# Output projections of a hybrid decoder trunk in weight blocks of 512 rows by 512 columns

## The chip, the cores and the metric

The kernel runs on one core of one Trainium2 chip. The metric is the device time of one execution in microseconds (us), as the median of the runs. The core's engines are TensorE (PE, matmuls), VectorE (DVE), ScalarE (ACT), GpSimd (POOL) and SyncE (SP, which here issues nearly all transfers). Each runs its own list of instructions in order and waits on semaphores for the others.

## What is computed

A trunk of two residual layers and a final RMSNorm on x of 1024 tokens by 1024 channels, in float32. Each layer ends with an output projection, and that is what the change is about:

```python
def rmsnorm(x, w):
    xf = x.astype(jnp.float32)
    y = xf * lax.rsqrt(jnp.mean(xf * xf, axis=-1, keepdims=True) + EPS)
    return (y * w.astype(jnp.float32)).astype(x.dtype)
```

Layer 0 joins an SSD branch (1024 channels, RMS-normed over all of them) and a differential attention branch (8 heads of 128) to y of 2048 channels; layer 1 is an HGRN2 recurrence with 16 heads of 128, again 2048 channels. Then x = x + y @ w_out with w_out of 2048 rows by 1024 columns, and layer 1 (or the final norm) starts from the RMS norm of that x.

## The kernel before

**Exact products.** Every float32 operand is split into two float32r parts, hi (a cast on ACT) and lo (the difference, on DVE). A product takes three matmuls: hi by hi, hi by lo, lo by hi. In `mm_tm` (matmuls on line 168) the stationary side is 128 channels by 128 tokens of y, the moving side 256 columns of the weights; in `mm_cm` (line 158), used by the input projections, the stationary side is a weight tile and the moving side 512 tokens. Weights come in blocks of 1024 rows by 256 columns through `_wprep`: two transfers of 512 KB into "w_raw" (line 110), two casts into "w_hi" (line 116), two differences into "w_lo" (line 117); "w_hi" and "w_lo" have two buffers each.

**Buffers.** Tiles are taken by tag from a table `SLOTS`, and tiles of all phases share the slots: "A" has 11 of 4 KB per partition, "V" four, "bt", "ey" and "th" one each. A tile can be filled only when the last reader of the slot's tile before is done. PSUM has two banks "pj", two "s1" and two pairs "big".

**The output projection** is `out_proj` (from line 652), called once a layer. The rows of y are transposed tiles of 128 channels by 512 tokens (a half `hf` of the tokens) that were stored in DRAM; `load_y` loads one (into "th" or, for odd tiles of half 1, "ey") or two at once (into "w_raw") and splits them. Part A takes channel tiles 0 to 7, which are there early (in layer 0 the SSD branch), for all tokens: four weight blocks `cb`, per block and half an x1 tile of 512 tokens by 256 columns, loaded from x (line 667) and updated with the sums (line 676 in layer 1; line 680 in layer 0, where the SSD branch's row scale is applied here). Part B takes channel tiles 8 to 15, for half 0 and then half 1, four weight blocks each, so that these blocks are loaded twice. Its sums are added on line 720, squares follow on ACT (723), and the row scale (734) ends in `finish`. In layer 0 `finish` stores x1 and makes layer 1's normed and transposed input; in layer 1 it scales the rows by the final norm and stores them.

**Order.** The code is written in program order and a tile scheduler puts every engine's list together, ahead of time. It draws part A's matmuls into the last heads, where PE would wait for softmax or state updates: they are filler there. A head ends in tail transposes (line 600 in the attention), the product with the gate and a store of its y (`emit_y`, lines 627 and 628). In an HGRN head the running state `st` is in "bt": a copy (1057) and updates (1059) on DVE, and the products with the state on PE (1066), beside the products within the chunk (1064).

## Time and profile before

| | us |
|---|---|
| median of three runs | 2345.65 (2345.0 to 2347.86) |
| the profiled execution, span | 2346.1 |
| PE busy in it | 2262.1 |
| DVE, ACT, POOL busy | 1269.5, 824.8, 187.5 |

The profile is of one execution. An engine's busy time is the union of its instructions; a matmul's listed duration overlaps its neighbours', so that the distance from start to start is its price in a stream. "Releaser" is what ended a wait. Windows give the busy time between two moments, and the granted clock of PE as a share of its full speed: 1.00 is 2.4 GHz and 0.50 is 1.2 GHz.

### The profile page before, as it was taken

The page shows a single profiled execution, that of the slowest core. Times are in us where ns is not written, and L with a number is a line of the kernel's source. Part 1 is how long each engine was busy: PE and PEld are TensorE (multiplying, and loading weights), DVE is VectorE, ACT ScalarE, POOL GpSimd, SP SyncE. Part 2 cuts the span into 40 slices and gives each one's busy share as a digit, 9 for nine tenths or more (in the row PEclk, how much of TensorE's full clock was granted, in tenths as well). Part 3 has the DMA queues.
Part 4 walks back from the last instruction along what each step waited for, and adds up shares of the span by engine and source line. Part 5 has one row for each costly group of instructions (what it writes and reads, how often), then busy time and mean ns, then how long its engine had stood idle before and what let it go on. Part 6 is the DMA issues. An engine that isn't in the chain of part 4 may idle for free.

```text
span 2346.1 us, 40804 instructions
## 1 busy us (share of the span) xinstructions
PE 2262.1 (96%) x16868; PEld 1927.1 (82%) x16868; DVE 1269.5 (54%) x2838; ACT 824.8 (35%) x1887; POOL 187.5 (8%) x201
## 2 busy tenths in 40 slices
PE   6959989899999999999999999999999999999998
PEld 4747766788778787788998888888888888989998
DVE  4736657535554545665444355555646465557444
ACT  4413333224444444544343223332323232334233
POOL 1000111100000000000001010101011010100000
PEclk9979999999999999999999999999999999999999
DMA  5342323231211211231432111111111111124323
GB/s 131 63 78 69 94 73 85 60 82 37 50 46 36 50 39 52 82 128 37 156 123 85 37 55 54 47 46 46 46 46 46 46 50 42 55 65 153 123 94 126
DMA packets 180701, 166.29 MB, mean 71 GB/s; under 512 B 9431, under 2 KB 162401, under 8 KB 180516
## 3 DMA queue, kind: packets, MB, share of 16 engines
q1 hardware_dynamic: 173668, 152.42, 21.5%
q0 software_dynamic: 2624, 7.08, 2.0%
q10 hardware_dynamic: 4224, 4.19, 0.5%
q8 instruction: 132, 2.16, 0.4%
q14 instruction: 53, 0.43, 0.1%
HBM read 132.66 MB, written 26.80 MB: 68 GB/s over the span
## 4 chain that ended last, share of the span: by engine, by line
PE 83%; DMA 10%; DVE 4%; ACT 2%; issue 1%; SPq 0%; POOL 0%; ACTq 0%; POOLq 0%; DVEq 0%
PE pj L158 38%; PE pj L168 21%; DMA G<-acs_d 6%; PE big L545 5%; PE big L168 5%; PE s L581 3%; PE big L976 2%; DMA tz_d<-o 1%; PE s L577 1%; PE big L1064 1%; PE big L1066 1%; PE s L1053 1%; DVE G L442 1%; PE big L1018 1%; DVE w_lo L117 1%
## 5 line engine op out<-in xcount | busy, mean ns | idle before, releaser
L158 PE MATMUL pj<-u,w_hi 128*128 128x512 f32 x3072 | 988.4, 399 | 12.2 <-ACT A L397 8.5
L158 PEld LDWEIGHTS pj<-u,w_hi 128*128 128x128 f32 x3072 | 570.4, 189 | 136.5 <-ACT A L397 9.7
L158 PE MATMUL pj<-u,w_lo 128*128 128x512 f32 x1536 | 609.7, 397 | 0.0
L168 PE MATMUL pj<-w_hi,u 128*128 128x256 f32 x2592 | 496.5, 287 | 1.0 <-DVE A L206 1.0
L168 PEld LDWEIGHTS pj<-w_hi,u 128*128 128x128 f32 x2592 | 409.6, 191 | 9.5 <-issue 5.6
L168 PE MATMUL pj<-w_lo,u 128*128 128x256 f32 x1296 | 370.2, 286 | 0.0
L158 PEld LDWEIGHTS pj<-u,w_lo 128*128 128x128 f32 x1536 | 290.2, 189 | 61.4 <-issue 2.2
L117 DVE TENSOR_TENSOR w_lo<-w_raw,w_hi 128x1024 fp32r<-128x1024 f32 x168 | 204.6, 1240 | 104.4 <-ACT w_hi L116 104.2
L168 PEld LDWEIGHTS pj<-w_lo,u 128*128 128x128 f32 x1296 | 248.0, 191 | 1.7 <-issue 0.6
L116 ACT CAST w_hi<-w_raw 128x1024 fp32r<-128x1024 f32 x168 | 168.0, 1046 | 200.2 <-PE pj L158 113.7
L545 PE MATMUL big<-A 128*128 128x512 f32 (+7 forms) x384 | 142.0, 420 | 0.0
L206 DVE SCALAR_TENSOR_TENSOR A<-th,pj 128x512 f32<-128x512 f32 x80 | 55.0, 688 | 143.9 <-ACT th L205 143.3
L205 ACT ACTIVATE th<-pj 128x512 f32<-128x512 f32 x96 | 57.2, 596 | 207.5 <-PE pj L158 202.7
L559 ACT ACTIVATE p<-p,mx 128x256 f32<-128x256 f32 (+7 forms) x128 | 98.7, 772 | 84.2 <-DVE mx L555 76.4
L545 PEld LDWEIGHTS big<-A 128*128 128x128 f32 (+1 forms) x384 | 71.2, 185 | 58.9 <-issue 50.6
L132 POOL TENSOR_TENSOR ro<-rs_t,mhalf 128x4 f32<-128x4 f32 x48 | 53.2, 1109 | 828.3 <-DVE rs_t L131 663.3
L579 ACT COPY wT<-s 128x512 f32<-128x512 f32 (+2 forms) x96 | 45.9, 478 | 134.4 <-PE s L577 133.9
L442 DVE TENSOR_SCALAR G<-G,ph 128x128 f32<-128x128 f32 x128 | 28.9, 287 | 108.1 <-DMA G<-acs_d 108.1
L893 POOL TENSOR_SCALAR A<-th,fN,fB 128x512 f32<-128x512 f32 x32 | 47.6, 1488 | 470.0 <-ACT th L890 470.0
L581 PE MATMUL s<-V,wT 128*128 128x128 f32 x576 | 81.2, 277 | 0.0
L960 DVE TENSOR_TENSOR A<-A,p 128x512 f32<-128x512 f32 x96 | 65.7, 685 | 23.5 <-PE big L976 23.0
L581 PEld LDWEIGHTS s<-V,wT 128*128 128x128 f32 x576 | 73.8, 191 | 4.5 <-issue 1.6
(328 smaller groups left out, 3030.7 us busy)
## 6 DMA issues: line engine op xcount, KB each, us to landing
w_raw<-in_even_w_in SPq DMA_DIRECT2D x32, 512.0 KB, 4.7
w_raw<-in_odd_w_in SPq DMA_DIRECT2D x64, 256.0 KB, 3.5
w_raw<-in_odd_w_in SPq DMA_DIRECT2D x32, 512.0 KB, 3.9
w_raw<-in_even_w_in SPq DMA_DIRECT2D x48, 256.0 KB, 3.9
w_raw<-in_even_w_out SPq DMA_DIRECT2D x24, 512.0 KB, 4.4
w_raw<-in_odd_w_out SPq DMA_DIRECT2D x24, 512.0 KB, 5.2
G<-acs_d SPq DMA_DIRECT2D x32, 256.0 KB, 4.7
yo<-ey SPq DMA_DIRECT2D x32, 256.0 KB, 2.0
```

The lines of the kernel that those rows point to most:

```text
L116: nc.scalar.copy(hq, raw)
L117: nc.vector.tensor_tensor(lq, raw, hq.bitcast(F32), op=ALU.subtract)
L132: nc.gpsimd.tensor_tensor(dst, t[:, :n], self.mhalf[:, :n], op=ALU.pow)
L158: nc.tensor.matmul(out, lhsT=ww[:, k, ms], rhs=uu[k][:, sl], start=(n == 0), stop=(n == 3 * KT - 1))
L168: nc.tensor.matmul(out, lhsT=uu[k], rhs=ww[:, k, :], start=(k == 0 and j == 0), stop=(k == KT - 1 and j == 2))
L205: nc.scalar.activation(th, pj, AF.Tanh, scale=0.5)
L206: nc.vector.scalar_tensor_tensor(out, view(th), 1.0, view(pj), op0=ALU.add, op1=ALU.mult)
L442: nc.vector.tensor_scalar(R[:, h], R[:, h], S.acs[:, c, 4 * g + h:4 * g + h + 1], 0.0, op0=ALU.subtract, op1=ALU.min)
L545: nc.tensor.matmul(s[:, k0:k0 + kn], lhsT=q[:, isl], rhs=k[:, k0:k0 + kn], start=(j == 0), stop=(j == 1))
L559: nc.scalar.activation(p[:, :n], p[:, :n], AF.Exp, bias=mx, accum_out=z)
L581: nc.tensor.matmul(po[:, i % 4, :], lhsT=wT[:, j * P:j * P + P], rhs=V(j, hh), start=(j == 0), stop=(j == i))
L960: nc.vector.tensor_tensor(k, k, bc(halves(Ts[h], 1)[1], [P, L // (2 * h), h]), op=ALU.mult)
```

## The change

Both projections go through w_out in eight blocks of 512 rows by 512 columns: four row groups `kq` of four channel tiles, two column halves `n`. A sum has 12 matmuls of 512 moving columns, where it had 24 of 256, and is added to x1 after every `kq`, so that each row of x1 is updated four times. The x1 tiles hold 256 tokens by 512 columns. `kq` 0 and 1 run over all tokens in "pj" banks, 2 over all tokens in "big" banks (two token tiles to an eviction). For `kq` 3 both blocks stay on chip, and the tokens go by halves; squares are taken of 512 columns, and in layer 1 each row is scaled and stored as soon as its second column half is done (`finish.row`). Each weight block is loaded once, 8 a layer in place of 12. The x1 tiles keep their list of tags; in the list's last place, "bt", stands now the last tile of the first row group.

```diff
@@ -94,25 +94,27 @@
         n, b = BANKS[tag]
         return self.pp.tile(shape or [P, n * 512], F32, name=tag, tag=tag, bufs=b)
     def _wprep(self, i):
         if i >= len(self.wspecs) or i in self.wtiles:
             return
         nc = self.nc
         src, row0, cols = self.wspecs[i]
-        hi = self.t("w_hi", [P, KT, WB], F32R)
-        lo = self.t("w_lo", [P, KT, WB], F32R)
+        wid = sum(n for _, n in cols)
+        kt = KT * WB // wid
+        hi = self.t("w_hi", [P, kt, wid], F32R)
+        lo = self.t("w_lo", [P, kt, wid], F32R)
         for q in range(2):
-            raw = self.t("w_raw", [P, KT // 2, WB])
-            k0 = q * (KT // 2)
+            raw = self.t("w_raw", [P, kt // 2, wid])
+            k0 = q * (kt // 2)
             o = 0
             for c0, n in cols:
                 nc.sync.dma_start(
                     raw[:, :, o:o + n],
-                    src[row0 + k0 * P:row0 + (k0 + KT // 2) * P, c0:c0 + n].rearrange(
+                    src[row0 + k0 * P:row0 + (k0 + kt // 2) * P, c0:c0 + n].rearrange(
                         "(k p) n -> p k n", p=P))
                 o += n
-            hq, lq = hi[:, k0:k0 + KT // 2, :], lo[:, k0:k0 + KT // 2, :]
+            hq, lq = hi[:, k0:k0 + kt // 2, :], lo[:, k0:k0 + kt // 2, :]
             nc.scalar.copy(hq, raw)
             nc.vector.tensor_tensor(lq, raw, hq.bitcast(F32), op=ALU.subtract)
         self.wtiles[i] = (hi, lo)
@@ -159,16 +161,17 @@
                                  start=(n == 0), stop=(n == 3 * KT - 1))
                 n += 1
-    def mm_tm(self, out, w, uh, ul, ks=range(KT)):
+    def mm_tm(self, out, w, uh, ul):
         nc = self.nc
         wh, wl = w
-        for k in ks:
+        kt = len(uh)
+        for k in range(kt):
             for j, (uu, ww) in enumerate(((uh, wh), (uh, wl), (ul, wh))):
                 nc.tensor.matmul(out, lhsT=uu[k], rhs=ww[:, k, :],
-                                 start=(k == 0 and j == 0), stop=(k == KT - 1 and j == 2))
+                                 start=(k == 0 and j == 0), stop=(k == kt - 1 and j == 2))
 @@ -650,92 +653,78 @@
 def out_proj(S, y_d, wcols, x_d, x1_tags, rs_a, finish):
     nc = S.nc
-    part = lambda y, t: [[z[:, i, t * P:t * P + P] for z in y] for i in range(2)]
     load = lambda hf, k, *tags: load_y(S, y_d, wcols, hf, k, tags)
-    ya, yb = [[], []], [[], []]
+    y = [[], []]
+    part = lambda kq, hf, t: [[z[:, i, t * P:t * P + P] for z in y[hf][4 * kq:4 * kq + 4]] for i in range(2)]
     for hf in range(2):
         for k in range(0, KT, 2):
-            ya[hf] += load(hf, k, "u", "u")
-    x1s = [], []
-    for cb in range(4):
+            y[hf] += load(hf, k, "u", "u")
+    x1s = {}
+    tags = iter(x1_tags)
+    for kq in range(2):
+        for n in range(2):
+            w = S.wnext()
+            for hf in range(2):
+                for t2 in range(2):
+                    if kq == 0:
+                        x1 = x1s[hf, n, t2] = S.t(next(tags), [P, 2, 512])
+                        r0 = hf * 512 + t2 * 256
+                        nc.sync.dma_start(x1, x_d[r0:r0 + 256, n * 512:n * 512 + 512].rearrange(
+                            "(t p) n -> p t n", p=P))
+                    x1 = x1s[hf, n, t2]
+                    for t in range(2):
+                        pa = S.ps("pj")
+                        S.mm_tm(pa, w, *part(kq, hf, 2 * t2 + t))
+                        if rs_a is None:
+                            nc.vector.tensor_tensor(x1[:, t], pa, x1[:, t], op=ALU.add)
+                        else:
+                            tok = hf * 4 + 2 * t2 + t
+                            nc.vector.scalar_tensor_tensor(x1[:, t], pa, rs_a[:, tok:tok + 1], x1[:, t],
+                                                           op0=ALU.mult, op1=ALU.add)
+            if kq == 1 and n == 0:
+                for k in range(KT, KT + 6, 2):
+                    y[0] += load(0, k, "A", "A")
+    for k in range(KT + 6, KT + 8):
+        y[0] += load(0, k, "u")
+    for k in range(8):
+        y[1] += load(1, KT + k, ("V", "V", "G", "G", "p0", "p0", "p1", "wT")[k])
+    for n in range(2):
         w = S.wnext()
         for hf in range(2):
-            x1 = S.t(x1_tags[2 * cb + hf], [P, 4, WB])
-            nc.sync.dma_start(x1, x_d[hf * 512:hf * 512 + 512, cb * WB:cb * WB + WB].rearrange(
-                "(t p) n -> p t n", p=P))
-            x1s[hf].append(x1)
             for t2 in range(2):
-                pa = S.ps("pj", [P, 2, WB])
-                ts_ = slice(2 * t2, 2 * t2 + 2)
+                pb = S.ps("big", [P, 2, 512])
                 for t in range(2):
-                    S.mm_tm(pa[:, t], w, *part(ya[hf], 2 * t2 + t))
-                if rs_a is None:
-                    nc.vector.tensor_tensor(x1[:, ts_], pa, x1[:, ts_], op=ALU.add)
+                    S.mm_tm(pb[:, t], w, *part(2, hf, 2 * t2 + t))
+                x1 = x1s[hf, n, t2]
+                nc.vector.tensor_tensor(x1, pb, x1, op=ALU.add)
+    ws = [S.wnext(), S.wnext()]
+    for hf in range(2):
+        ss = S.sm.tile([P, 4, 2], F32, name="ss4", bufs=2)
+        rows = [x1s[hf, n, t2] for n in range(2) for t2 in range(2)]
+        rss = []
+        for n in range(2):
+            for t in range(4):
+                pa = S.ps("pj")
+                S.mm_tm(pa, ws[n], *part(3, hf, t))
+                xr = x1s[hf, n, t // 2][:, t % 2]
+                nc.vector.tensor_tensor(xr, pa, xr, op=ALU.add)
+                jk = S.t("th", [P, 512])
+                nc.scalar.activation(jk, xr, AF.Square, accum_out=ss[:, t, n:n + 1])
+                if n == 1:
+                    sr = S.sm.tile([P, 1], F32, name="sr")
+                    nc.vector.tensor_tensor(sr, ss[:, t, 0:1], ss[:, t, 1:2], op=ALU.add)
+                    rs = S.sm.tile([P, 1], F32, name="rs")
+                    S.rstd(rs, sr, 1.0 / D, EPS)
+                    rss.append(rs)
+                    finish.row(hf, t, [x1s[hf, m, t // 2][:, t % 2] for m in range(2)], rs)
                 else:
-                    for t in range(2):
...
+                    finish.early(xr)
+        finish(hf, x1s, rss)
 def wspecs(a):
@@ -752,7 +741,7 @@
             specs.append((W, 0, [(AG0 + h * P, WB)]))
         elif h < 7:
             specs.append((W, 0, [(AV0 + (h + 1) * P, WB)]))
-    out = lambda w: [(w, half * D, [(cb * WB, WB)]) for half in (0, 1, 1) for cb in range(4)]
+    out = lambda w: [(w, kq * 512, [(n * 512, 512)]) for kq in range(4) for n in range(2)]
     l0 = specs + out(WO)
     W, WO = a["odd_w_in"][0], a["odd_w_out"][0]
     specs = []
@@ -801,25 +790,30 @@
     nc = S.nc
     def finish(hf, x1s, rs):
-        for cb, x1 in enumerate(x1s):
-            nc.scalar.dma_start(x1_d[hf * 512:hf * 512 + 512, cb * WB:cb * WB + WB].rearrange(
-                "(t p) n -> p t n", p=P), x1)
+        for n in range(2):
+            for t2 in range(2):
+                r0 = hf * 512 + t2 * 256
+                nc.scalar.dma_start(x1_d[r0:r0 + 256, n * 512:n * 512 + 512].rearrange(
+                    "(t p) n -> p t n", p=P), x1s[hf, n, t2])
+        for cb in range(4):
             if hf == 0:
                 xn = [S.t("o", [P, 2, WB]) for _ in range(2)]
             else:
                 xn = S.t("G", [P, 4, WB])
                 xn = [xn[:, 0:2], xn[:, 2:4]]
             for t in range(4):
+                src = x1s[hf, cb // 2, t // 2][:, t % 2, (cb % 2) * WB:(cb % 2) * WB + WB]
                 if t % 2:
-                    nc.scalar.activation(xn[t // 2][:, t % 2], x1[:, t], AF.Copy, scale=rs[t])
+                    nc.scalar.activation(xn[t // 2][:, t % 2], src, AF.Copy, scale=rs[t])
                 else:
-                    nc.vector.tensor_scalar(xn[t // 2][:, t % 2], x1[:, t], rs[t], None, op0=ALU.mult)
+                    nc.vector.tensor_scalar(xn[t // 2][:, t % 2], src, rs[t], None, op0=ALU.mult)
             for j in range(2):
                 k = 2 * cb + j
                 if u[0] is None:
                     u[0], u[1] = S.alloc_u()
                 S.u_block(u, k, hf, [xn[t // 2][:, t % 2, j * P:j * P + P] for t in range(4)], wcol[:, k:k + 1])
-    finish.early = None
+    finish.early = lambda xr: None
+    finish.row = lambda hf, t, x1, rs: None
     return finish
@@ -907,35 +901,30 @@
     for i in range(2):
         fw = S.t("o", [P, 512])
         nc.gpsimd.dma_start(fw, bc(a["final_norm_w"][i * 512:i * 512 + 512].unsqueeze(0), [P, 512]))
-        fws += [fw[:, 0:WB], fw[:, WB:]]
...
+        fws.append(fw)
+    def early(xr):
+        nc.vector.tensor_tensor(xr, xr, fws[0], op=ALU.mult)
+    def row(hf, t, x1, rs):
+        o = S.t("u", [P, D])
+        nc.scalar.activation(o[:, 0:512], x1[0], AF.Copy, scale=rs)
+        nc.vector.scalar_tensor_tensor(o[:, 512:], x1[1], rs, fws[1], op0=ALU.mult, op1=ALU.mult)
+        r0 = hf * 512 + t * P
+        nc.sync.dma_start(out[r0:r0 + P, :], o)
     def finish(hf, x1s, rs):
-        for t in range(4):
...
+        pass
+    finish.early, finish.row = early, row
     out_proj(S, lambda k, n: yo[k:k + n], None, x1_d, ["V", "V"] + ["A"] * 5 + ["bt"], None, finish)
```

Comments taken away by the change are left out here. The two sides of three places in the engines' lists:

PE at the end of layer 0's last head, before. L600 are the last tail transposes (s1_8677); behind and ahead of them are sums of half 0, and the last values stand 65 matmuls further up.

```order
L168 MATMUL pj_9660<-w_hi_9427,A_9424 128x256
L168 MATMUL pj_9660<-w_lo_9428,A_9424 128x256
L168 MATMUL pj_9660<-w_hi_9427,A_9424 128x256
L168 MATMUL pj_9660<-w_hi_9427,u_9647 128x256
L600 MATMUL s1_8677<-ident_71,o_8658 128x128 x4
L168 MATMUL pj_9660<-w_lo_9428,u_9647 128x256
L168 MATMUL pj_9660<-w_hi_9427,u_9647 128x256
L168 MATMUL pj_9660<-w_hi_9427,u_9706 128x256
L168 MATMUL pj_9660<-w_lo_9428,u_9706 128x256
```

The same place now. L584 are the last values (wT_8637), L603 the tail transposes; V_9289, V_9294, G_9299 and G_9304 are channel tiles 8 to 11 of half 1.

```order
L584 MATMUL s1_8515<-V_7030,wT_8637 128x128 x4
L171 MATMUL big_9389<-w_hi_9155,V_9289 128x512
L171 MATMUL big_9389<-w_lo_9156,V_9289 128x512
L171 MATMUL big_9415<-w_hi_9155,V_9289 128x512
L171 MATMUL big_9415<-w_lo_9156,V_9289 128x512
L171 MATMUL big_9389<-w_hi_9155,V_9289 128x512
L171 MATMUL big_9415<-w_hi_9155,V_9289 128x512
L603 MATMUL s1_8677<-ident_71,o_8658 128x128 x4
L171 MATMUL big_9389<-w_hi_9155,V_9294 128x512
L171 MATMUL big_9389<-w_lo_9156,V_9294 128x512
L171 MATMUL big_9415<-w_hi_9155,V_9294 128x512
L171 MATMUL big_9415<-w_lo_9156,V_9294 128x512
```

Between the last values and the transposes there are now six matmuls, and what follows the transposes takes channel tile 9 (V_9294) of half 1; all products of the second column half with half 0's tiles, which were loaded earlier, come later in the list.

SP, the same place before. yb_75<-ey_8682 is the store of the last head's y, th and ey are loads of half 1's channel tiles.

```order
L636 DMA th_10165<-yb_75 128x512
L110 DMA w_raw_9786<-in_even_w_out 128x4x256
L110 DMA w_raw_9790<-in_even_w_out 128x4x256
L628 DMA yb_75<-ey_8682 128x512
L636 DMA ey_9779<-yb_75 128x512
L636 DMA ey_9916<-yb_75 128x512
L110 DMA w_raw_9903<-in_even_w_out 128x4x256
L110 DMA w_raw_9907<-in_even_w_out 128x4x256
```

Now, with ey_9292 for V_9294 and ey_9302 for G_9304:

```order
L112 DMA w_raw_9443<-in_even_w_out 128x2x512
L112 DMA w_raw_9447<-in_even_w_out 128x2x512
L639 DMA th_9297<-yb_75 128x512
L639 DMA th_9307<-yb_75 128x512
L631 DMA yb_75<-ey_8682 128x512
L639 DMA th_9317<-yb_75 128x512
L639 DMA ey_9292<-yb_75 128x512
L639 DMA ey_9302<-yb_75 128x512
```

The loads into "ey" stand behind the store on both sides. Before, all of half 0's part-B products lay between them and their use on PE; now it is the products shown above.

DVE at the end of layer 1's last head, before. bt_19911 is the head's state, pj the part-A sums.

```order
L1057 COPY bt_19911<-s1_19923 128x128
L1059 SCALAR_TENSOR_TENSOR bt_19911<-bt_19911,p1_19730,s1_19923 128x128 x3
L676 TENSOR_TENSOR A_20395<-pj_20397,A_20395 128x512
L1059 SCALAR_TENSOR_TENSOR bt_19911<-bt_19911,p1_19730,s1_19932 128x128 x3
L131 TENSOR_SCALAR rs_t_19965<-so_19955 128x4
L1077 TENSOR_TENSOR o_19968<-big_19939,ro_19964 128x512
```

Now, with bt_19105 for the state, and bt_19493 for the x1 tile that takes its slot:

```order
L1046 COPY bt_19105<-s1_19117 128x128
L119 TENSOR_TENSOR w_lo_19524<-w_raw_19525,w_hi_19523 128x1024
L1048 SCALAR_TENSOR_TENSOR bt_19105<-bt_19105,p1_18924,s1_19117 128x128
L119 TENSOR_TENSOR w_lo_19524<-w_raw_19529,w_hi_19523 128x1024
L1048 SCALAR_TENSOR_TENSOR bt_19105<-bt_19105,p1_18924,s1_19117 128x128 x2
L1048 SCALAR_TENSOR_TENSOR bt_19105<-bt_19105,p1_18924,s1_19126 128x128 x3
L650 TENSOR_TENSOR A_19647<-w_raw_19645,A_19647 128x512
L650 TENSOR_TENSOR A_19650<-w_raw_19645,A_19650 128x512
L650 TENSOR_TENSOR A_19655<-w_raw_19653,A_19655 128x512
L650 TENSOR_TENSOR A_19658<-w_raw_19653,A_19658 128x512
L133 TENSOR_SCALAR rs_t_19159<-so_19149 128x4
L684 TENSOR_TENSOR bt_19493<-pj_19495,bt_19493 128x512
L684 TENSOR_TENSOR bt_19493<-pj_19509,bt_19493 128x512
```

Two differences of a weight block (L119) stand now between the state updates (L1048), and the first sums for the tile in "bt" come right behind, ahead of the head's own scaling (L1066); before, "bt" was taken up as the last of the x1 tiles. On PE these two sums (pj_19495, pj_19509) are the last filler ahead of the state products, and hold both "pj" banks.

## Rows read from the trace of the kernel before

**Rows 1.** The page, busy times: engine, us (share of the span) xinstructions.

```profile
PE 2262.1 (96%) x16868; PEld 1927.1 (82%) x16868; DVE 1269.5 (54%) x2838; ACT 824.8 (35%) x1887; POOL 187.5 (8%) x201
```

**Rows 2.** The page, costliest groups: line engine operation | busy, mean ns | idle, releaser.

```profile
L168 PE MATMUL pj<-w_hi,u 128*128 128x256 f32 x2592 | 496.5, 287 | 1.0 <-DVE A L206 1.0
...
L117 DVE TENSOR_TENSOR w_lo<-w_raw,w_hi 128x1024 fp32r<-128x1024 f32 x168 | 204.6, 1240 | 104.4 <-ACT w_hi L116 104.2
...
L116 ACT CAST w_hi<-w_raw 128x1024 fp32r<-128x1024 f32 x168 | 168.0, 1046 | 200.2 <-PE pj L158 113.7
```

**Rows 3.** Timeline of PE, 256 moving columns: start us, us, engine, line, operation.

```profile
2266.28 0.28 PE L168 MATMUL big<-w_lo,A 128*128 128x256 f32 x1
...
2266.64 0.28 PE L168 MATMUL big<-w_lo,A 128*128 128x256 f32 x1
```

**Rows 4.** Timeline of PE, 512 moving columns, an input projection of layer 1.

```profile
2083.64 0.39 PE L158 MATMUL pj<-u,w_lo 128*128 128x512 f32 x1
...
2084.32 0.39 PE L158 MATMUL pj<-u,w_lo 128*128 128x512 f32 x1
```

**Rows 5.** Windows: from:to, length, busy us of each engine, PEclk, DMA share, GB/s.

```profile
core 0: us, PE busy (x) PEld busy (x) DVE busy (x) ACT busy (x) POOL busy (x), PEclk, DMA share, GB/s
950.00:1140.00 190.00, 190.00 (x1274) 162.90 (x1273) 117.82 (x351) 90.65 (x218) 7.46 (x8) 1.00 0.30 97
1174.00:1176.00 2.00, 0.41 (x2) 0.19 (x1) 1.74 (x3) 2.00 (x3) 0.00 (x0) 1.00 0.00 0
1176.00:1178.00 2.00, 1.31 (x7) 1.26 (x7) 2.00 (x3) 1.05 (x5) 0.00 (x0) 0.74 0.70 227
1178.00:1180.00 2.00, 2.00 (x12) 2.00 (x11) 0.42 (x1) 1.02 (x4) 0.00 (x0) 0.50 0.99 286
2174.00:2195.00 21.00, 21.00 (x212) 20.62 (x212) 8.24 (x21) 2.71 (x8) 0.00 (x0) 1.00 0.01 4
2270.00:2280.00 10.00, 10.00 (x86) 10.00 (x85) 4.94 (x6) 3.94 (x10) 0.00 (x0) 1.00 0.34 105
```

**Rows 6.** Timelines of PE, DVE, SP and ACT, end of layer 0's last head.

```profile
1138.31 1.06 PE L581 MATMUL s<-V,wT 128*128 128x128 f32 x8
...
1142.55 0.17 DVE L131 TENSOR_SCALAR rs_t<-so 128x4 f32<-128x4 f32 x1 [0.48 <-ACT junk L592]
...
1147.00 0.60 PE L600 MATMUL s<-ident,o 128*128 128x128 f32 x4
...
1149.36 1.23 SPq L628 DMA_DIRECT2D yb<-ey  x1
1155.04 4.43 SPq L636 DMA_DIRECT2D ey<-yb  x2
...
1157.78 0.62 ACT L646 CAST V<-ey 128x512 fp32r<-128x512 f32 x1 [7.45 <-DMA ey<-yb]
```

**Rows 7.** DMA issues, the whole span: out<-in queue xcount, KB each, median us to landing.

```profile
A<-x_d SPq DMA_DIRECT2D x5, 512.0 KB, 6.6
...
yb<-ey SPq DMA_DIRECT2D x16, 256.0 KB, 2.0
...
ey<-yb SPq DMA_DIRECT2D x4, 256.0 KB, 2.8
...
V<-x_d SPq DMA_DIRECT2D x2, 512.0 KB, 3.4
```

**Rows 8.** Timelines of DVE and SP, end of layer 1's last head and later.

```profile
2188.40 0.29 DVE L1057 COPY bt<-s 128x128 f32<-128x128 f32 x1 [4.56 <-PE s L1053]
2188.72 1.12 DVE L1059 SCALAR_TENSOR_TENSOR bt<-bt,p,s 128x128 f32<-128x128 f32 x3
...
2194.47 0.36 SPq L667 DMA_DIRECT2D bt<-x_d  x1
...
2240.96 0.68 DVE L676 TENSOR_TENSOR bt<-pj,bt 128x512 f32<-128x512 f32 x1
```

**Rows 9.** Timeline of DVE, the last sum taken up at the kernel's end.

```profile
2339.39 0.42 DVE L720 TENSOR_TENSOR bt<-pj,bt 128x256 f32<-128x256 f32 x1
```

71 lines of the change are left out of this document (removed).

## The prediction

> **What bounds the kernel now.** I read the page's busy times and slices first [rows 1]: TensorE (PE) is busy for 2262.1 of 2346.1 us, VectorE for 1269.5 and ScalarE for 824.8. So an edit is worth what it takes from PE's stream or what idle time it puts into it. Next came the costliest groups [rows 2] and, for the price of one instruction, the timeline of PE, since a group's mean of overlapped instructions (287 ns) is not a rate: from the first row to the second in [rows 3], three matmuls of 256 moving columns start in 0.36 us, 0.12 us each; in [rows 4], three of 512 columns start in 0.68 us, 0.2267 us each. The windows [rows 5] tell where PE has no gap: it is busy for 190.00 of 190.00 us in the attention stage from 950 to 1140 and for 21.00 of 21.00 around the end of the last HGRN head. There the part-A sums of the output projection fill every wait. The change rewrites this filler, so the question is whether the new filler still covers.
>
> The profiled execution spans 2346.1 us, 0.45 more than the median of the three runs, 2345.65. The sum is made against 2346.1, and 0.45 is taken off at the end.
>
> **The columns: a gain.** Each projection has 24 matmuls for each of 8 token tiles in 8 weight blocks (A and both halves' B count the same products): 1536 of 256 columns in a layer become 768 of 512. One pair costs 2 x 0.12 = 0.24, its successor 0.2267: 0.0133 us less, 1536 pairs in the two layers, **-20.4 us**, wherever PE is the bound. The window at 2270 says why two short ones cost more than one long one: weight loads (PEld) are busy for 10.00 of 10.00 us there [rows 5].
>
> A rule of the Trainium skill speaks against this term. "TensorE: Matmul & The Clock Gate", section "Back-to-back issue gap", gives N / 2.4 + 2.5 ns for a warm matmul, which would make 109.2 and 215.8 ns and so 2.6 ns for a pair, 4.0 us in all. The rows differ from it (120 and 227 ns), and the measurement decides.
>
> **Weights: nothing.** Twelve weight blocks a layer become eight. Eight blocks fewer spare 16 casts of 1.046 us on ScalarE and 16 splits of 1.240 us on VectorE [rows 2], 16.7 and 19.8 us, on engines that are busy for 35% and 54% [rows 1]. Gone cover costs nothing here, and neither do wider evictions, one for two.
>
> **Fewer entries into the filler: -2 us.** The scheduler cuts a run of filler about 30 times less often in the heads' ends. No row isolates what one entry costs; it is at most the 0.12 us in which a whole matmul starts after another [rows 3], so 0 to 3.6, and I take 2.
>
> **Attention, heads 5 to 7: +4 us.** Between tail transposes of two half heads the order has, in five successive stretches, 136, 157, 159, 142 and 193 filler matmuls before and 72, 48, 132, 108 and 78 after. By their rates that is 16.3, 18.8, 19.1, 17.0, 23.2 us before, and 16.3, 10.9, 29.9, 24.5, 17.7 after. A part-A sum over only four channel tiles uses a row tile of x1 for 24 matmuls, 5.4 us, so the tiles run out sooner, and the next x1 tile waits for a buffer that the head's scores hold. The second stretch loses 7.9 us of cover. How much of this was needed the trace can't show, as PE never stopped [rows 5]: 0 to 7.9, plus nothing for the stretches with more. I take 4.
>
> **Layer 0, end of the last head: +12.4 us.** In the row chain of before [rows 6] the last values end at 1139.37, the row scale comes at 1142.55, the tail transposes at 1147.00, and the store of the gated result is issued at 1149.36. The first "ey" load can be issued at 1155.04 and is cast at 1157.78, done 0.62 later: 19.0 us after the last values. PE worked through it all, on 46 part-A matmuls, then on half 0's blocks, which need none of these channels. In the new order only six matmuls stand between the last values and the tail transposes, and behind these come products with V_9294 and G_9304 for half 1, which pass through the one "ey" buffer after the head's own store. The 48 free matmuls of the next column block stand behind them in PE's queue and cannot pass. Upper bound: 19.0 less 6 x 0.2267 less 0.6 for the transposes, 17.0. Lower: the store needs 2.0 us in place of 5.7 (its common time, [rows 7]) and the transposes do not stand behind filler (1.5 less): 11.8. The second load, G_9304, takes 2.8 [rows 7] plus cast, against 12 matmuls that cover 2.7 of it: 1.5 more. I take 13.5 of 13.3 to 18.5, low, since nothing large is loaded just ahead of the store. After the idle time the clock: before, PE was busy for 0.41 of 2 us at 1174, then the granted clock was 0.74 and 0.50 in two windows of 2 us [rows 5]. Half is the 1.2 GHz level; over both windows 0.76 x 2 = 1.5 us of PE's work are lost. A longer gap should bring the same, and 12 matmuls between two gaps at half rate: 2.7. Before had 2.3 idle (1.59 in the first window, 0.69 in the second) and these 1.5, 3.8. Net 13.5 + 2.7 - 3.8.
>
> **Layer 1, end of the last head: +12.2 us.** Before, filler stands among the state products, so PE is never idle [rows 5]. In the new order the last filler block ahead of them ends one weight block, and that releases a buffer: two splits of 1.24 us [rows 2] stand between the state updates on VectorE, each behind its cast of 1.05. Updates take 0.29 for the first and 0.37 each for six [rows 8]: with the first cast done at 1.15, the chain is 1.2 + 1.24 + 0.37 + 1.24 + 5 x 0.37 = 5.9, and the last state product ends about 6.35 after the filler. PE has 0.7 of values and 1.45 of small products in it: 4.2 idle. Then it wants a "pj" bank; both hold sums of the x1 tile in "bt", and that buffer was the heads' state. Its load is issued only when the last state product has read it. In before the same load was issued at 2194.47 and its sum taken up at 2240.96, 46 us later [rows 8]: there "bt" was the last column block's; now it is in the first of four passes. A load of x1 takes 3.4 to 6.6 [rows 7], and the eviction 0.68: 4.1 to 7.3 idle; I take 6.4, as other loads share that moment. Half clock for 3 us as above: 1.6. Sum 4.2 + 6.4 + 1.6, bounds 8 to 15.
>
> **The end: +0.5 us.** The last sum of 256 columns is taken up in 0.42 [rows 9], and a square and a scaling follow. With 512 columns it takes 0.68, as the same operation in [rows 8]; the others grow too, while rows that are written as they come leave fewer pieces. 0 to 1.
>
> Sum: -20.4 - 2 + 4 + 12.4 + 12.2 + 0.5 = +6.7, so 2352.8, less 0.45: **2352 us**. The turn between the layers I cost at nothing: by the order, 35 matmuls (8 us by 0.2267) of half 1 stand over half 0's last eviction, square, scale and transposes, which together are some 3.5 us if each takes the 0.4 to 0.7 of [rows 8, 9]; without that cover it would cost these 3.5.
>
> **The rivals.**
> 1. *The gaps are small, faster.* PE's place in the order tells what comes next, not when: if x1's last tile and the "ey" loads are on chip within half of what I count, because the SP queue reaches them early, the two ends cost 6 each, the attention nothing: -20.4 - 2 + 12 + 0.5 = -9.9, **2336**. For it: every load above has a short form in the trace (2.8, 3.4 in [rows 7]). Against: both loads wait for a buffer whose last reader is named in the order, no queue can send them sooner. The three stalls, 28.6 us in my sum, decide: at 21.9 together the kernel is as fast as before, under 17 it is faster by more than 0.2%. Chance 0.20.
> 2. *The loads run into each other, slower still.* In [rows 6] a store of 256 KB took 5.7 us to land where weight loads ran. With such times the ends cost 17.4 and 15, attention 7.9: -20.4 - 1 + 17.4 + 15 + 7.9 + 1 = +19.9, **2366**. Chance 0.15.
> 3. *A 512-column matmul brings nothing.* [Rows 4] were read in an input projection, where weights are the stationary side. If in the output projection one long matmul took as long as two short ones, 0.24 us, all of the 20.4 us would be missing: **2372**. Against it: nothing in the two forms differs but the names of the sides. Chance 0.03. By the rule of the Trainium skill above, 4.0 of the 20.4 would be left, 2368.
>
> **How the numbers follow.** My forecast, gaps as counted, has 0.62, from 2343 to 2359. A difference under 0.2%, 4.7 us, can hardly be told from none. About half of the forecast's case lies under 2350.3, the upper half above. Faster 0.20 (rival 1, nearly all of it below 2341), same 0.30, slower 0.50 (0.32 of the forecast, rivals 2 and 3). The range, 2338 to 2364, leaves out the lower part of rival 1, the upper of rival 2, and rival 3.
>
> **What would show it.** The columns: 128x512 rows of the output projection 0.227 us apart. Layer 0: a PE gap of 10 us or more from the last values to a DVE split of an "ey" tile, and a granted clock of 0.5 behind it. Layer 1: a gap at the last state products, released by a w_lo split, then one released by the load of bt. Attention: PE idle between the last tail of the sixth head and the first of the seventh, with x1 loads as releasers. If PE is busy throughout at both ends, rival 1 holds and my reading of the order was wrong; if no gap is there and time is not lower, the column term is.

## The result: 2361.8 us, slower by 0.6%, within the range and over the forecast

| | us |
|---|---|
| before, median of 4 runs | 2345.32 (2343.26 to 2347.86) |
| after, median of 4 runs | 2361.82 (2357.96 to 2362.98) |
| after by before | 1.0063, 95% interval 1.0048 to 1.0077 |
| profiled execution after, span | 2360.9 (before 2346.1) |

The forecast was 2352 with 2338 to 2364: the sign is right, the time lies in the range, and the loss is 14.8 us by the spans and 16.5 by the medians, where 6.7 were summed. First the page of after, whose first line answers to [rows 1] and whose groups answer to [rows 2]:

```profile
PE 2255.4 (96%) x15332; PEld 1852.1 (78%) x15332; DVE 1288.9 (55%) x2838; ACT 800.3 (34%) x1799; POOL 187.7 (8%) x201
...
L171 PE MATMUL pj<-w_hi,u 128*128 128x256 f32 (+1 forms) x2112 | 490.7, 320 | 12.1 <-DVE bt L684 5.5
...
L119 DVE TENSOR_TENSOR w_lo<-w_raw,w_hi 128x1024 fp32r<-128x1024 f32 x152 | 185.5, 1243 | 96.0 <-ACT w_hi L118 95.6
...
L118 ACT CAST w_hi<-w_raw 128x1024 fp32r<-128x1024 f32 x152 | 152.1, 1047 | 209.7 <-PE pj L160 113.2
```

PE is busy for 6.7 us less than before in a span that is 14.8 longer. It isn't PE's work that grew, its waits did; and in L171's group the idle time ahead of it, 1.0 us before, is now 12.1, of which 5.5 are released by the taking up of x1's tile bt (L684). Casts and splits went from 168 to 152, the 16 that were counted.

**The columns.** A timeline of PE in the output projection, after (start, us, engine, line, operation), as [rows 3, 4]:

```profile
2300.86 0.39 PE L171 MATMUL big<-w_hi,G 128*128 128x512 f32 x1
2301.08 0.39 PE L171 MATMUL big<-w_lo,G 128*128 128x512 f32 x1
2301.31 0.62 PE L171 MATMUL big<-w_hi,G 128*128 128x512 f32 x2
2301.76 0.39 PE L171 MATMUL big<-w_lo,G 128*128 128x512 f32 x1
```

From one w_lo row to the next there are three matmuls in 0.68 us, 0.227 each, as in the input projection of before.

**Where PE waits.** The same three windows of both kernels (length, busy us of each engine, PEclk, DMA share, GB/s), of before:

```profile
core 0: us, PE busy (x) PEld busy (x) DVE busy (x) ACT busy (x) POOL busy (x), PEclk, DMA share, GB/s
980.00:1060.00 80.00, 80.00 (x550) 69.48 (x549) 53.20 (x152) 39.08 (x93) 3.82 (x4) 1.00 0.43 139
1160.00:1250.00 90.00, 87.00 (x696) 85.45 (x695) 40.55 (x69) 40.62 (x97) 3.82 (x7) 0.98 0.44 138
2140.00:2250.00 110.00, 110.00 (x1120) 108.64 (x1119) 61.06 (x115) 33.86 (x80) 5.15 (x6) 1.00 0.44 144
```

and of after:

```profile
980.00:1060.00 80.00, 73.24 (x340) 55.59 (x339) 52.74 (x145) 39.28 (x92) 3.07 (x4) 0.96 0.48 149
1160.00:1250.00 90.00, 79.55 (x357) 65.09 (x356) 36.77 (x55) 29.02 (x64) 3.19 (x5) 0.92 0.26 88
2140.00:2250.00 110.00, 101.01 (x737) 82.45 (x737) 73.58 (x138) 38.62 (x90) 6.84 (x7) 0.97 0.45 146
```

The first is the sixth and seventh head of the attention, the second the end of layer 0's last head, the third the end of layer 1's last head. What PE lost in a window is its idle time and, while it worked at a low clock, its busy time times what the clock lacks of 1.00; a low clock in which PE stands costs nothing more. The stretches at a low clock in these windows, three of after:

```profile
1008.00:1014.80 6.80, 6.17 (x16) 4.93 (x17) 4.50 (x13) 2.03 (x6) 0.00 (x0) 0.50 0.31 105
1168.40:1182.10 13.70, 6.67 (x17) 5.14 (x18) 3.80 (x6) 2.47 (x4) 0.00 (x0) 0.50 0.29 97
2216.30:2223.20 6.90, 4.64 (x11) 3.67 (x12) 4.33 (x9) 3.43 (x16) 2.01 (x2) 0.51 0.47 147
```

and one of before:

```profile
1176.90:1180.40 3.50, 3.50 (x18) 3.50 (x19) 1.52 (x2) 1.19 (x6) 0.00 (x0) 0.51 0.99 301
```

Before: 0; 3.0 idle + 1.7 by the clock; 0. After: 6.8 + 3.1 = 9.9; 10.5 + 3.3 = 13.8; 9.0 + 2.3 = 11.3. So the three places cost 9.9, 9.1 and 11.3, 30.3 together, against 28.6 in the sum. With -20.4 for the columns that would make +9.9, but the two spans differ by 14.8.

The rest lies in PE's own stream, that is the span less PE's idle time and less what the low clock cost. In the whole span PE idles for 84.0 us before and 105.5 after, and it is busy at the low clock for 29.2 and 45.5 us, which costs 14.6 and 22.8. That leaves a stream of 2247.5 us before and 2232.6 after: 14.9 less, not 20.4.

The waits themselves, PE's timeline after, with the idle time ahead of each and its releaser in brackets. At the end of layer 0's last head:

```profile
1168.82 1.09 PE L603 MATMUL s<-ident,o 128*128 128x128 f32 x4 [3.81 <-DVE o L598]
1176.52 0.79 PE L171 MATMUL big<-w_hi,V 128*128 128x512 f32 x1 [6.61 <-ACT V L649]
...
1182.17 0.39 PE L171 MATMUL big<-w_lo,G 128*128 128x512 f32 x1
```

and the queues beside it (the store of the head's result, the ey loads behind it, the cast that releases PE):

```profile
1170.73 0.32 SPq L631 DMA_DIRECT2D yb<-ey  x1
1172.79 8.90 SPq L639 DMA_DIRECT2D ey<-yb  x3
...
1175.85 0.62 ACT L649 CAST V<-ey 128x512 fp32r<-128x512 f32 x1 [0.31 <-DMA ey<-yb]
```

The chain is the one of the prediction: store issued at 1170.73, ey load at 1172.79 (so the store took 2.1 us at most), cast at 1175.85. The row at 1176.52 is the product with that tile, after 6.61 us. The transposes ahead had 3.81 of their own. From 1168.4 to 1182.1 the granted clock is 0.50, the 1.2 GHz level (row above); PE stands for half of that time and works at half speed for the other half.

At the end of layer 1's last head, PE, then DVE, then SP, after, answering to [rows 8]:

```profile
2209.44 0.49 PE L1055 MATMUL big<-bt,p 128*128 128x128 f32 x2 [0.66 <-DVE bt L1048]
2210.83 0.49 PE L1055 MATMUL big<-bt,p 128*128 128x128 f32 x2 [0.68 <-DVE bt L1048]
2218.56 0.79 PE L171 MATMUL pj<-w_hi,u 128*128 128x512 f32 x1 [5.46 <-DVE bt L684]
...
2207.91 1.22 DVE L119 TENSOR_TENSOR w_lo<-w_raw,w_hi 128x1024 fp32r<-128x1024 f32 x1
2209.04 0.34 DVE L1048 SCALAR_TENSOR_TENSOR bt<-bt,p,s 128x128 f32<-128x128 f32 x1
2209.30 1.22 DVE L119 TENSOR_TENSOR w_lo<-w_raw,w_hi 128x1024 fp32r<-128x1024 f32 x1
...
2213.14 0.36 SPq L677 DMA_DIRECT2D bt<-x_d  x1
...
2217.82 1.29 DVE L684 TENSOR_TENSOR bt<-pj,bt 128x512 f32<-128x512 f32 x2
```

The two splits (1.22 us) stand between the state's updates, but cost PE only 0.66 and 0.68. The x1 load is issued at 2213.14, its sums are taken up from 2217.82, and PE waits 5.46 for that.

In the attention, PE and the transfer it waits for, after:

```profile
999.66 0.66 PE L580 MATMUL s<-ident,p 128*128 128x128 f32 x4 [1.55 <-ACT wT L582]
1008.63 0.80 PE L171 MATMUL pj<-w_hi,u 128*128 128x512 f32 x1 [3.71 <-DVE V L687]
...
1001.24 0.37 SPq L677 DMA_DIRECT2D V<-in_x  x1
...
1007.82 1.41 DVE L687 SCALAR_TENSOR_TENSOR V<-pj,rsa,V 128x512 f32<-128x512 f32 x2 [3.43 <-DMA V<-in_x]
```

The first wait has too little filler ahead of it. The second is filler with nowhere to put its sum: the x1 tile in "V" is asked for at 1001.24, when the head's values have left the slot, and lands 6.6 us later; PE has by then filled both "pj" banks, and the clock is at 0.50 after it. How long PE stands here varies from execution to execution. In e1, e2, e6 and e7 (twice) of the next section, whose order is the same in these heads, the wait for this tile is 4.6, 1.6, 2.2, 1.9 and 1.8 us, and the window costs 10.2, 6.4, 6.9, 8.0 and 6.9. With after's 9.9 the mean is 8.0.

### The profile page after: what moved, and what is told of

Read it like the earlier page. It is cut to its first block, busy times and chain, and to the rows that moved or that the text cites. A ratio compares the mean times of both kernels' runs of the same rounds, so it can differ in the third digit from the quotient of the medians.

```text
span 2360.9 us, 37579 instructions
## 1 busy us (share of the span) xinstructions
PE 2255.4 (96%) x15332; PEld 1852.1 (78%) x15332; DVE 1288.9 (55%) x2838; ACT 800.3 (34%) x1799; POOL 187.7 (8%) x201
## 3 DMA queue, kind: packets, MB, share of 16 engines
q1 hardware_dynamic: 152932, 144.03, 20.4%
## 4 chain that ended last, share of the span: by engine, by line
PE 80%; DMA 11%; DVE 5%; ACT 2%; issue 1%; SPq 0%; POOL 0%; POOLq 0%; DVEq 0%; ACTq 0%
PE pj L160 38%; PE pj L171 21%; DMA G<-acs_d 6%; PE big L548 5%; PE big L171 4%; PE s L584 3%; PE big L965 2%; DMA tz_d<-o 1%; PE s L580 1%; PE big L1053 1%; DVE G L445 1%; PE s L1042 1%; PE big L1055 1%; PE big L1007 1%; DMA A<-in_x 1%
## 5 line engine op out<-in xcount | busy, mean ns | idle before, releaser
L160 PE MATMUL pj<-u,w_hi 128*128 128x512 f32 x3072 | 990.3, 400 | 10.4 <-ACT A L400 7.3
L171 PE MATMUL pj<-w_hi,u 128*128 128x256 f32 (+1 forms) x2112 | 490.7, 320 | 12.1 <-DVE bt L684 5.5
L171 PEld LDWEIGHTS pj<-w_hi,u 128*128 128x128 f32 x2112 | 354.2, 192 | 44.1 <-DVE bt L684 5.6
L171 PE MATMUL pj<-w_lo,u 128*128 128x256 f32 (+1 forms) x1056 | 333.7, 316 | 0.0
L119 DVE TENSOR_TENSOR w_lo<-w_raw,w_hi 128x1024 fp32r<-128x1024 f32 x152 | 185.5, 1243 | 96.0 <-ACT w_hi L118 95.6
L118 ACT CAST w_hi<-w_raw 128x1024 fp32r<-128x1024 f32 x152 | 152.1, 1047 | 209.7 <-PE pj L160 113.2
L171 PEld LDWEIGHTS pj<-w_lo,u 128*128 128x128 f32 x1056 | 202.8, 192 | 11.3 <-issue 0.2
L584 PE MATMUL s<-V,wT 128*128 128x128 f32 x576 | 81.1, 278 | 0.8 <-ACT wT L582 0.8
L584 PEld LDWEIGHTS s<-V,wT 128*128 128x128 f32 x576 | 74.7, 191 | 6.7 <-issue 1.5
```

Of the source, the lines that this page charges most:

```text
L118: nc.scalar.copy(hq, raw)
L119: nc.vector.tensor_tensor(lq, raw, hq.bitcast(F32), op=ALU.subtract)
L160: nc.tensor.matmul(out, lhsT=ww[:, k, ms], rhs=uu[k][:, sl], start=(n == 0), stop=(n == 3 * KT - 1))
L171: nc.tensor.matmul(out, lhsT=uu[k], rhs=ww[:, k, :], start=(k == 0 and j == 0), stop=(k == kt - 1 and j == 2))
L584: nc.tensor.matmul(po[:, i % 4, :], lhsT=wT[:, j * P:j * P + P], rhs=V(j, hh), start=(j == 0), stop=(j == i))
```

## The experiments

All times are medians. They come from three sets of runs, in which the kernel before took 2346.4 (e1, e2, e3, e6), 2346.1 (e4, e5, e7, e9) and 2345.7 (e10, e11, e7 again). To tell the layers apart in one execution, I also use three stretches between instructions that all kernels have: A from the tail transposes at about 980 to layer 1's first input projection, B from there to the tail of head 14, C from there to the end.

| kernel | median us | by before (95%) | A | B | C |
|---|---|---|---|---|---|
| before | 2345.3 | | 266.6 | 914.2 | 185.4 |
| after | 2361.8 | 1.0063 (1.0048 to 1.0077) | 276.3 | 915.5 | 188.4 |
| e1 half 0 first | 2359.4 | 1.0052 (1.0037 to 1.0067) | 273.5 | 915.6 | 190.7 |
| e2 bt late | 2347.8 | 1.0007 (0.9997 to 1.0016) | 272.4 | 915.8 | 179.2 |
| e3 first in A | 2360.7 | 1.0061 (1.0045 to 1.0076) | 271.8 | 916.8 | 191.7 |
| e6 raw in o | 2350.6 | 1.0015 (1.0005 to 1.0025) | 264.0 | 916.4 | 189.0 |
| e7 = e2 + e6 | 2339.4 | 0.9977 (0.9965 to 0.9989) | 266.2 | 916.2 | 179.0 |
| e7 again | 2339.3 | 0.9968 (0.9957 to 0.9978) | 264.4 | 915.7 | 177.7 |
| e5 = e7, all in 256 columns | 2352.0 | 1.0023 (1.0013 to 1.0032) | 264.0 | 915.6 | 189.8 |
| e4 = e7 + e3 | 2341.4 | 0.9978 (0.9967 to 0.9989) | 263.8 | 915.6 | 178.7 |
| e9 = e7, pairs of row groups | 2361.7 | 1.0068 (1.0051 to 1.0085) | 271.9 | 917.8 | 189.0 |
| e10 = e7, layer 0's group 0 in 256 | 2340.1 | 0.9972 (0.9961 to 0.9983) | 263.1 | 915.6 | 181.7 |
| e11 = e7, layer 0's groups 0, 1 in 256 | 2334.8 | 0.9955 (0.9942 to 0.9969) | 260.7 | 916.5 | 179.6 |

A, B and C are of one execution each. The A of after, e1, e2 and e3 differ by up to 4.5 us, and in after and e2, which have the same layer 0, by 3.9; the C of the six executions with e2's layer 1 (e2, e4, e7 twice, e10, e11) lie between 177.7 and 181.7. So a difference of 4 us in one stretch is not clear by itself. The execution of e7 that was traced first was its longest, 9.2 us over the median; some 5 of these lie ahead of A, where all these kernels are the same.

**e1_half0_first.** The order of the third row group's products:

```diff
-    for n in range(2):
-        w = S.wnext()
-        for hf in range(2):
+    ws = [S.wnext(), S.wnext()]
+    for hf in range(2):
+        for n in range(2):
```

> The third row group takes half 0 with both column blocks first, then half 1, so that the 48 matmuls of the second block that need none of the last head's channels stand ahead of the products with the channel tiles loaded through ey. Theory A (the gap is the chain last values - store - ey load - split, which begins with the last values): the scheduler only draws these 48 matmuls ahead of the last values, the chain begins 10.9 us later, PE idles as long as now, 10.4 us between 1158 and 1178 of the changed kernel's trace, and the time stays within 3 us of 2361.8. Theory B (the free work stands in the wrong place): it fills the gap, 8 to 10 us less, about 2352.

Measured: 2359.4, 2.4 us less. Theory A: free work was drawn ahead (17 matmuls in place of 6 stand between the last values and the tail transposes), and the gap came later, between 1174 and 1184, with 8.0 us in place of 10.4, as a chain does that begins with the last values. My prediction had named both the load and the 48 free matmuls that "cannot pass" as the reason; the second is not one.

**e2_bt_late.** Only layer 1's tags:

```diff
-                    y[0] += load(0, k, "A", "A")
+                    y[0] += load(0, k, "A", y_last if k == KT + 4 else "A")
...
-    out_proj(..., ["V", "V"] + ["A"] * 5 + ["bt"], None, finish)
+    out_proj(..., ["V", "V"] + ["A"] * 6, None, finish, "bt")
```

> In layer 1 the last x1 tile takes an A slot in place of bt, and the channel tile 13 of half 0, needed only in the last row group, takes bt. Theory A (the load of x1 that waits for the state's buffer holds both pj banks): the filler comes back among the state products, PE's 9.0 us of idle time and 3.5 us of lost clock between 2150 and 2250 go, 2361.8 - 12 = about 2350. Theory B (the two weight splits between the state updates are the cause, or another x1 tile takes the place of bt): at most 3 us less, 2359 or more.

Measured: 2347.8, 14.1 less; in C, which is layer 1's, 188.4 became 179.2 (the mean of the six executions named above is 179.3, that of after, e1, e3 and e6 190.0: 10.6 less). Theory A. The third window, e2:

```profile
2140.00:2250.00 110.00, 108.41 (x750) 89.68 (x749) 73.75 (x137) 36.44 (x86) 6.84 (x7) 0.98 0.48 156
```

PE is busy for 108.41 in place of 101.01; the two w_lo splits moved out from between the state updates too, as filler stands there again, so that this run by itself doesn't tell the two apart; that the splits cost 1.3 us of after's waits and the tile in "bt" 5.5 is read from the rows of after above.

**e3_first_in_A.** One tag in layer 0:

```diff
-             ["V", "V", "bt"] + ["A"] * 5, rsa,
+             ["A", "V", "V", "bt"] + ["A"] * 4, rsa,
```

> In layer 0 the list of x1 tags begins with A in place of V, so that the first x1 tile is loaded before the attention's values have left the V slots. Theory A (the filler of the sixth head stands still because its first sum cannot be added to an x1 tile whose load is issued at 1001.2 and lands at 1007.8): the 5.3 us of idle time and the 3.5 us of lost clock between 996 and 1016 go, or most of it, 2361.8 - 7 = about 2355. Theory B (the same tiles only run out one sum later): less than 3 us, 2359 or more.

Measured: 2360.7, 1.1 less, and with the ends repaired (e4) no gain over e7. Theory B by the time. The first window's idle time fell from 6.8 to 2.7 us, but its clock stayed at 0.96, and it still costs 6.1:

```profile
980.00:1060.00 80.00, 77.27 (x359) 58.32 (x359) 55.61 (x150) 39.85 (x94) 3.07 (x4) 0.96 0.49 152
```

That is just under the 6.4 to 10.2 of the kernels without this edit, a gain too small for these runs. PE's longest wait there is now 1.30 us, for scales of the softmax from DVE at 1008.46, and the next x1 tile's load came at 1005.40 in place of 1001.24, behind others in SP's queue.

**e6_raw_in_o.** The buffer of layer 0's odd channel tiles:

```diff
-    raw = S.t("w_raw" if n == 2 else (("th", "ey")[k % 2] if hf else "th"), [P, n, 512])
+    raw = S.t("w_raw" if n == 2 else (("th", "o" if wcols is not None else "ey")[k % 2] if hf else "th"), [P, n, 512])
```

> In layer 0 the odd channel tiles of half 1 are loaded through the two o slots in place of the one ey slot that the last head's result is stored from. Theory A (the ey buffer holds up the products behind the tail transposes): the load no longer waits for the store; left is the wait for the V and G slots and for th, 2 to 3 us; 10.4 us of idle time and some 4 us of clock at half become about 4, so 2361.8 - 9 = about 2353. Theory B (the V and G slots that the last head frees are what the splits wait for, the raw buffer is not): within 3 us of 2361.8.

Measured: 2350.6, 11.2 less, and only A became shorter. Theory A. The second window, e6:

```profile
1160.00:1250.00 90.00, 86.19 (x396) 70.58 (x395) 45.11 (x77) 35.86 (x79) 5.95 (x10) 1.00 0.33 108
```

Idle 3.8 in place of 10.5, and the clock never falls: the window costs 3.8 in place of 13.8.

**e7_bt_and_o**, both, no new edit.

> Both repairs that showed an effect together: layer 1's last x1 tile in an A slot (as in e2_bt_late) and layer 0's odd channel tiles of half 1 through the o slots (as in e6_raw_in_o). Theory A (the stalls are separate and each is paid in full): 2361.8 - 14.1 - 11.2 = about 2336.5, under the kernel before by 0.4%. Theory B (time freed at one place is lost at the next wait): 2343 or more.

Measured: 2339.4, and 2339.3 in a second set of runs (e7_again), 22.4 under after; 25.3 would be the sum of the two. Nearer to theory A: the two places are separate to within some 3 us, about what the intervals leave open, and in both sets this kernel is faster than before by its interval.

**e5_two_256.** e7 with

```diff
-        for k in range(kt):
-            for j, (uu, ww) in enumerate(((uh, wh), (uh, wl), (ul, wh))):
-                nc.tensor.matmul(out, lhsT=uu[k], rhs=ww[:, k, :],
...
+        for c in range(0, wh.shape[-1], WB):
+            for k in range(kt):
+                for j, (uu, ww) in enumerate(((uh, wh), (uh, wl), (ul, wh))):
+                    nc.tensor.matmul(out[:, c:c + WB], lhsT=uu[k], rhs=ww[:, k, c:c + WB],
```

> As e7_bt_and_o, but each product of 512 moving columns is issued as two of 256, one column half after the other, in the same bank and the same blocks. Only the number and width of the output projections' matmuls differ from e7. Theory A (0.24 us for a pair against 0.2267): 0.0133 x 1536 = 20.4 us over e7, less what falls into waits, so 15 to 20 more. Theory B (N / 2.4 + 2.5 ns, the rule of the Trainium skill, TensorE: Matmul & The Clock Gate, Back-to-back issue gap): 4 us more.

Measured: 12.6 over e7, between the theories. The stretches tell why: in C, where idle time and low clock cost about the same in both (10.0 and 9.7), the short matmuls cost 10.8 more (189.8 against 179.0), and 768 pairs by 0.0133 are 10.2. In A they cost nothing (264.0 against 266.2 and 264.4), because there the waits are gone. The rows of the first window, e7, then e5:

```profile
980.00:1060.00 80.00, 75.16 (x351) 57.56 (x350) 55.78 (x156) 39.52 (x93) 3.68 (x5) 0.96 0.44 141
```

```profile
980.00:1060.00 80.00, 78.08 (x525) 66.65 (x524) 56.90 (x157) 41.79 (x98) 3.07 (x4) 1.00 0.46 153
```

With short filler the first window lost 1.9 us and no clock; with long filler 4.8 and 3.2 (6.9 in all in e7 again). In the second window e5 lost nothing and e7 5.4 (3.8 in e7 again). In the order, e5's filler between tail transposes is 129, 115, 161, 145, 205 short matmuls, 15.5, 13.8, 19.3, 17.4 and 24.6 us, where e7 has 16.3, 10.9, 29.9, 24.5 and 20.4: the scheduler spreads short ones more evenly, though they are less in sum (90.6 us against 102.0). The price of a pair was right, and the filler's width has a price of its own. A window of 80 us in each, late in layer 1, where PE does nothing else:

```profile
2260.00:2340.00 80.00, 79.75 (x352) 65.71 (x350) 38.17 (x58) 21.06 (x43) 3.82 (x7) 1.00 0.17 63
```

```profile
2260.00:2340.00 80.00, 80.00 (x669) 80.00 (x668) 33.42 (x50) 17.65 (x37) 2.75 (x5) 1.00 0.14 50
```

352 matmuls in 79.75 us are 0.227 each, 669 in 80.00 are 0.120, and with 256 columns the weight loads (second pair of numbers, PEld) have no gap, as in [rows 5]. The rule of the Trainium skill that the prediction weighed ("TensorE: Matmul & The Clock Gate", "Back-to-back issue gap", which gives it for a matmul by itself) would make 2.5 ns a pair, an estimate of 2 us in C. 10.8 were measured, so the rule does not give the price of this stream.

**e9_pairs_bt_o.** e7, with the first two row groups in one sum:

```diff
-    for kq in range(2):
-        for n in range(2):
-            w = S.wnext()
+    for n in range(2):
+        ws = [S.wnext(), S.wnext()]
...
-                        S.mm_tm(pa, w, *part(kq, hf, 2 * t2 + t))
+                        for q in range(2):
+                            S.mm_tm(pa, ws[q], *part(q, hf, 2 * t2 + t), q == 0, q == 1)
```

> As e7_bt_and_o, but the first two row groups are summed in one go: both weight blocks of a column half are on chip, a bank holds a sum of 24 matmuls of 512 columns, and each x1 tile is updated once there. Theory A (two open sums of 12 matmuls, 5.4 us, are too little cover for a wait on an x1 load in the attention, where before two banks held 96 short ones, 11.5 us): the idle time and half clock between 995 and 1016 go, 6 to 8 us under e7, about 2329. Theory B (the load of x1 comes late whatever the sums hold, or the change of two weight blocks at once costs as much): no less than e7 less 2, 2335 or more.

Measured: 2361.7, 22 over e7. Theory A fell. In the sixth head 38 matmuls of filler were left in the first stretch in place of 72. The wait for the x1 tile is gone there, but others took its place (3.9 us idle in the first window, with the clock at 0.94), and new waits arose at both ends and in the midst of the projection, where two weight blocks change at once. Two of them, e9:

```profile
1171.55 0.79 PE L171 MATMUL big<-w_hi,V 128*128 128x512 f32 x1 [3.83 <-ACT V L649]
...
2262.31 0.50 PE L171 MATMUL big<-w_hi,A 128*128 128x512 f32 x1 [3.79 <-ACT A L649]
```

Both wait for the cast of a channel tile (L649). How much each of its waits costs was not taken apart.

**e4_all_three**, e7 with e3's tag.

> As e7_bt_and_o, with layer 0's first x1 tile in an A slot (as in e3_first_in_A, whose idle time between 980 and 1060 was 4.0 us less while its time was only 1.2 less). Theory A (the gain is real and was lost to the clock elsewhere): 3 to 4 us under e7. Theory B (it is only moved): within 2 us of e7.

Measured: 2341.4, as e7 within the runs' spread: theory B by the time. That the wait only moves isn't shown: the first window costs 5.7, against 8.0 and 6.9 in the two executions of e7, a gain that these runs can't tell from none.

**e10_short_filler0, e11_short_filler01.** e7 with e5's pairs of 256 columns only where the filler is:

```diff
-                        S.mm_tm(pa, w, *part(kq, hf, 2 * t2 + t))
+                        S.mm_tm(pa, w, *part(kq, hf, 2 * t2 + t), WB if rs_a is not None and kq < 2 else None)
```

(`kq < 1` in e10; `rs_a` is given in layer 0 only.)

> As e7_bt_and_o, but in layer 0 the first row group's products, which are the filler of the sixth and seventh head, are issued as pairs of 256 moving columns; all others keep 512. The filler between the tail transposes changes from 72, 48, 132, 108, 90 matmuls to 129, 115, 152, 120, 126. Theory A (the thin and coarse filler is what costs the attention its 5 to 8 us): 192 pairs cost 192 x 0.0133 = 2.6 us more and 5 to 8 us of waits and half clock go, 2 to 5 us under e7. Theory B (the x1 load decides, whatever the filler's width): 2.6 us over e7.

> As e10_short_filler0, with the second row group of layer 0 in pairs of 256 columns as well. 384 pairs cost 5.1 us. Theory A: 2.6 us over e10, about as e7, since the sixth head's waits are gone in e10 already. Theory B (the later heads gain too): no more than e10.

> e7_bt_and_o once more, beside the two kernels that are compared with it. Both theories: 2337 to 2341, under the kernel before by 0.2 to 0.4%.

Measured in one set of runs: e7 2339.3, e10 2340.1, e11 2334.8. For e10 neither theory: it lost nothing and gained nothing. For e11 theory B: with the second row group's filler short as well it is 5.3 under e10, though that costs 2.6 more of PE. The single runs overlap (2331.9 to 2340.7, e10 2336.3 to 2344.6, e7 2335.0 to 2340.6), so the gain is likely, not certain. The traces agree with it: in A, idle time and low clock cost 13.4 and 10.7 us in e7's two executions, 8.0 in e10, 5.1 in e11 and 1.9 in e5. The second window, e11:

```profile
1160.00:1250.00 90.00, 90.00 (x418) 74.53 (x417) 39.92 (x68) 29.74 (x61) 5.53 (x10) 1.00 0.29 97
```

PE is busy for 90.00 of 90.00 and the clock is full. e11's order has 200 matmuls, 193 of them short (24.7 us), in the stretch up to the last tail transposes, e10 126 long ones (28.6) and e7 90 (20.4). So it isn't the amount of filler. What differs is where it stands: between the last values and the tail transposes there are 74 matmuls in e11 (65 before), 69 of them with channels that need no head of the attention, but 18 in e7 and e10, all with half 1's tiles in "V" and "G". In the first window e11 still idles for 1.7 us. With 2334.8 it is the fastest of all, 0.45% under before.

## Right and wrong, step by step

- **The columns, -20.4: the price of a pair right, the gain 14.9.** Between kernels that differ in the width alone the term holds: layer 1's C gives 10.8 for half of it; e5's whole stream, 2251.1 us, is 19 longer than e7's, 2231.7 and 2232.2; e11 against e5, which differ by 1152 pairs and share layer 0's filler, gives 17.3 where 15.4 are worked out. But e5, with matmuls as wide as before, has a stream 3.6 us longer than before. So something else in the new order costs PE some 4 us beside its visible waits. The prediction has no term for it, and its cause stays open.
- **Fewer entries, -2: not seen.** Whatever they gave, the rest of the stream grew.
- **Weights at nothing: nearly right.** 16 casts and splits fewer cost nothing and gave a little. Before, PE waited 2.4 us for splits in the projections (w_lo, L117; four waits of 0.5 to 0.7); after, for none there.
- **Layer 0's end, +12.4: the mechanism right, the size 9.1.** The gap was 10.4 idle in place of 13.5. The chain from the last values to the product took 12.9 us (1163.6 to 1176.5) where 13.8 were counted with the short store, PE had 2.5 of work in it in place of 2.0, and the second load's 1.5 did not come. The clock cost 3.3 after, in place of 2.7, and idle time and clock 4.7 before, in place of 3.8. e6 shows the cause, the one ey buffer; e1 shows that the order of the free products isn't one.
- **Layer 1's end, +12.2: near in sum, 11.3, not in its parts.** The chain through the splits took 5.8 us as worked out at 5.9 (from the filler's end at 2206.6 to 2212.4), but cost PE 1.3, not 4.2: PE's own work in it is 1.7 for the values and some 3.4 for the small products, where I had 0.7 and 1.45, having counted each product once, and the trace has two matmuls of each. The bt load cost 5.5 of 6.4 counted; the clock 2.3 in place of 1.6. The rest, 2.2, are waits that I left out: two at the tail of the head before (1.17 and 0.36 us, for an eviction and a row scaling) and two for later sums (0.47 and 0.19). e2 settles that the tags are the cause: with bt out of the first pass, some 11 us of C go, splits and all.
- **The attention, +4: mis-sized,** 9.9 in after, 8.0 in the mean of the six executions. The bound, 7.9 us, was the cover lost in the second stretch by counted filler. But PE stood in the first stretch, whose filler took 16.3 us before and after: the count says how much filler there is, not where it can be used. In the rows, 3.7 of the 6.8 idle are a wait for an x1 load of 6.6 us with both banks full, which the text names but does not price; and after it come 3.1 us by the half clock, which the sum held for the two ends only. What that load costs alone isn't shown, since e3 took its wait away and gained 1.1. That long matmuls make a worse filler was no term at all; e5 and e11 point to it.
- **The turn between the layers at nothing: right.** PE has no wait there (from 1177 to 1286).
- **The end, +0.5: right.** The last sum is taken up at 2353.87 of 2360.9, 7.0 us from the end; before 2339.39 of 2346.1, 6.7 ([rows 9]).

So the time lies 8.1 us over the sum by two terms that were too good, PE's stream (-14.9 for -22.4) and the attention (9.9 for 4), less some 5 that the two ends and the rest of the span came out under their terms. That it stays in the range is in part luck: the two terms that were too good would alone have brought the forecast's 2352 to 2365.

Of the rivals, 1 fell with the gaps and 3 with e5. Rival 2 gave 2366, nearer than the forecast to 2361.8, but not by its mechanism: neither end had loads that ran into each other (the store took 2.1 us at most, the bt load 4.7); the loss beyond the forecast is in the attention and in PE's stream.

Open is why the clock, at the same idle time, sometimes stays full (the first windows of e5 and e10 at 1.00, with 1.9 us idle) and sometimes not (0.96 in e4 with 2.3 idle and in e11 with 1.7); what adds some 4 us to PE's stream; and what exactly in the scheduler's costs spreads the short filler evenly.
